# Latent attention in a decoder block: normalized probabilities copied within SBUF and transposed as rounded 32-bit, scores three steps ahead

## The chip, the cores and the metric

The program runs on one core of a Trainium2 chip. The metric is device time of one execution in microseconds (us); lower is better. Three runs of the kernel before took 1321.53, 1325.11 and 1323.86 us, so their median is 1323.86. Engines go by the profile's names: PE multiplies matrices (PEld is its weight load), DVE, ACT and POOL work on vectors, SP issues most transfers. A transfer (DMA) is issued by an engine's instruction and landed by 16 DMA engines.

## The reference

One layer of a decoder block on 1024 tokens of width 1024 in float32: RMS norm, one projection, two attention mixers side by side (a sliding window of 128 keys, and latent attention), gates, an output projection, then a gated feed-forward. The change lies in the latent attention, 8 heads in blocks of 128 queries:

```python
s = (einsum('bqhd,bkhd->bhqk', qn, k_nope) + einsum('bqhr,bkr->bhqk', qr, k_rope)) * scale
s = where(causal, s, -inf)
p = softmax(s, axis=-1)
o = einsum('bhqk,bkhd->bqhd', p, v)
```

## The kernel before

**Products.** The kernel keeps float32 precision by splitting each operand into a rounded high part and a low rest (float32r, "rounded 32-bit", which PE takes at its quick pace) and adding three products: high by high, high by low, low by high. `split` (lines 163 and 166) makes the two parts: a copy on ACT, a subtraction on DVE. Rounded 32-bit operands have four bytes, like float32.

**Stages.** Norm and projections come first, then the sliding-window attention mixed with the gates' projection, then the latent projections, then the latent attention (the stage of the change), then the output products and the feed-forward. The sliding-window part already has a copy of its probabilities within SBUF (`per<-pe`, line 1095) and transposes them as rounded 32-bit (line 1008); so does the stage after it with the latents (`lT`, line 1118).

**The stage of the change.** A loop over t = 0 to 63 (8 heads, 8 query blocks each, in the order 2, 3, 6, 7, 0, 1, 4, 5). Block n of a head has (n+1) x 128 keys. `scores(t)` makes the scores on PE into a buffer `scb` of two PSUM banks, of which there are two buffers; DVE masks them and takes the row maximum (line 1263), ACT takes the exponential and the row sum (1264), POOL inverts the sum (1265) and scales the row (1266) into `p`. `transposes(t)` has PE turn each 128 x 128 block of `p` by a product with the identity matrix (1280) into a PSUM bank `pTb`, and `split` makes of it the halves `pth` and `ptl`. `pv` multiplies these with the values (1302, 1303) into `ob`. In one pass of the loop `scores(t + 2)` is called before `transposes(t)`. Other work fills the loop: products `oA` of the sliding-window output with its output matrix (lines 172 to 174 by `mm3`, ended on DVE at 1359), their weights' loads and splits (`wr`, `wv`), loads of the heads' queries and keys (`qT`, lines 1227 and 1230; `kT`, 1222), gate loads (`sg`, 1333), stores of finished rows (`ar_d`, 1364), and sums of blocks of the output matrix, made by transfers between DRAM tensors `wt_d` (lines 338 and 329).

**What sets the order.** Here no order is written out by hand: a scheduler places every engine's instructions when the program is built, by program order, its own estimate of when inputs are ready, and free slots. Once built, each engine goes through its list in order, and an instruction that has to wait holds up all that stands behind it. SP's list is such a list too, and all its transfers go out through one queue. Tiles called U share 21 slots of 4 KB a partition: `p`, `pth`, `ptl`, and the targets of most loads. PSUM has four banks for `pTb`, `ob`, `oA` and `k` together, and two double banks for `scb`.

Of the kernel before, what the change touches and what calls it, by code (L numbers as in the profile page):

```python
# [8 lines left out]
F32 = mybir.dt.float32  # L9
F32R = mybir.dt.float32r  # L10
# [7 lines left out]
P = 128  # L18
# [71 lines left out]
def hybrid_block_kernel(  # L90
# [29 lines left out]
    nc = tc.nc  # L120
# [9 lines left out]
    def psum_phase(name, bufs):  # L130
        if psum:
            psum.pop("cm").close()
        psum["cm"] = ExitStack()
        psum["x"] = psum["cm"].enter_context(tc.tile_pool(name=name, bufs=bufs, space=PSUM))
# [5 lines left out]
    def uid(name):  # L140
        counter[0] += 1
        return f"{name}_{counter[0]}"

    def U(name, dt=F32, shape=(P, 1024)):
        return pool.tile(list(shape), dt, tag="u", name=uid(name))

    def V(name, dt=F32, shape=(P, 4, 512)):
        return vpool.tile(list(shape), dt, tag="v", name=uid(name))

    def tiny(name, w=1):  # L150
        return small.tile([P, w], F32, tag=f"t{w}", name=uid(name))

    def P1(name, shape=(P, 512), dt=F32):
        return ps1.tile(list(shape), dt, tag="ps", name=uid(name))

    def PX(name, shape=(P, 512), dt=F32):
        return psum["x"].tile(list(shape), dt, tag="ps", name=uid(name))
# [3 lines left out]
    def split(hi, lo, src, eng=None):  # L161

        i = nc.scalar.copy(hi, src)  # L163
        if held[0]:
            tc.keep_in_program_order(i)
        (eng or nc.vector).tensor_tensor(lo, src, hi.bitcast(F32), op=ALU.subtract)  # L166

    def mm3(ps, pairs, first=True, last=True, go_on=False):

        n = len(pairs)  # L170
        for i, ((ah, al), (bh, bl)) in enumerate(pairs):
            nc.tensor.matmul(ps, ah, bh, start=first and i == 0, stop=False, skip_group_check=go_on)  # L172
            nc.tensor.matmul(ps, ah, bl, start=False, stop=False, skip_group_check=go_on)  # L173
            nc.tensor.matmul(ps, al, bh, start=False, stop=last and i == n - 1, skip_group_check=go_on)  # L174
# [7 lines left out]
    def blk(b, n=1):  # L182
        return slice(b * P, (b + n) * P)
# [5 lines left out]
    ident_r = const.tile([P, P], F32R, name="ident_r")  # L189
    ident = ident_r.bitcast(F32)  # L190
# [237 lines left out]
    for g in range(NG):  # L428
        t = V("khd", F32R, (P, 2, S))
# [486 lines left out]
    for b in range(NB):  # L916
# [17 lines left out]
        t = U("lat", F32, (P, C_CKV))  # L934
# [102 lines left out]
    for i, b in enumerate((4, 5, 6, 7, 0, 1, 2, 3)):  # L1037
        ps = P1("kl", (P, KVL))
        mm3(ps, [(hT(k, blk(b)), (wkl[k // 4][0][:, k % 4], wkl[k // 4][1][:, k % 4])) for k in range(NK)])
        t = U("lat", F32, (P, 2, KVL))  # L1040
# [104 lines left out]
    for s in range(2):  # L1145
        pr = P1("krT", (ROPE_B, 4, P), F32R)
        for j in range(4):
            nc.tensor.transpose(pr[:, j], lat[4 * s + j][:, C_RT:C_CKV], ident_r)
        pr = pr.bitcast(F32)
# [63 lines left out]
    def prod_v(b):  # L1213
        ps = P1("v")
        mm3(ps, [((ckv[k][0][:, blk(b)], ckv[k][1][:, blk(b)]), (wv[0][:, k], wv[1][:, k])) for k in range(2)])
        if b % 2 == 0:
            t = V("vM", F32R, (P, 2, NH, P))
            vM.extend([t[:, 0], t[:, 1]])
        split(vM[b][:, :, 0:HD], vM[b][:, :, HD:P], ps.rearrange("p (h d) -> p h d", d=HD))

    def load_k(h):
        nc.sync.dma_start(kT[h % 3][0:64].bitcast(F32), kn_d[h // 2, 64 * (h % 2):64 * (h % 2) + 64])

    def load_q(h):
        if h >= 2:
            qT[h] = V("qT", F32R, (P, 2, S))
            nc.sync.dma_start(qT[h][0:64].bitcast(F32), qn_d[h // 2, 64 * (h % 2):64 * (h % 2) + 64])
        t = qT[h]
        for i in range(2):
            nc.sync.dma_start(t[64 + 16 * i:80 + 16 * i].bitcast(F32), qr_d[i, 16 * h:16 * h + 16])  # L1230

    ob = {}
    live = {}
# [5 lines left out]
    def step(t):  # L1239
        return t // NB, order[t % NB]  # L1240

    def scores(t):
        h, n = step(t)
        w = (n + 1) * P
        sc = PX("scb", (P, 1024))
        qh, ql = (qT[h][0:QK, i] for i in range(2))
        kh, kl = (kT[h % 3][0:QK, i] for i in range(2))
        cw = 320 if w == 640 else 512
        for c0 in range(0, w, cw):
            c1 = min(c0 + cw, w)  # L1250
            kc = slice(c0, c1)
            o = slice(c0 // cw * 512, c0 // cw * 512 + c1 - c0)
            nc.tensor.matmul(sc[:, o], qh[:, blk(n)], kh[:, kc], start=True, stop=False)
            nc.tensor.matmul(sc[:, o], qh[:, blk(n)], kl[:, kc], start=False, stop=False)
            nc.tensor.matmul(sc[:, o], ql[:, blk(n)], kh[:, kc], start=False, stop=True)  # L1255
        nm = tiny("nmb")
        p = U("p")
        den = tiny("denb")
        s_, m_, p_ = sc[:, 0:w], mask[:, S - w:], p[:, 0:w]
        if cw == 320:  # L1260
            s_ = sc.rearrange("p (a c) -> p a c", a=2)[:, :, 0:320]
            m_, p_ = (v.rearrange("p (a c) -> p a c", a=2) for v in (m_, p_))
        nc.vector.tensor_tensor_reduce(s_, s_, m_, 1.0, -NEG, op0=ALU.add, op1=ALU.min, accum_out=nm)  # L1263
        nc.scalar.activation(p_, s_, AF.Exp, scale=-1.0, bias=nm, accum_out=den)  # L1264
        nc.gpsimd.tensor_tensor(den, den, neg_one[:, 0:1], op=ALU.pow)  # L1265
        nc.gpsimd.tensor_scalar(p[:, 0:w], p[:, 0:w], den, 0.0, op0=ALU.mult, op1=ALU.add)  # L1266
        live[t] = p

    def transposes(t):
        h, n = step(t)  # L1270
        p = live.pop(t)
        j, odd = divmod(n, 2)
        if not odd:
            pts[(h, j)] = [(U("pth", F32R, (P, 4, 256)), U("ptl", F32R, (P, 4, 256)))
                           for _ in range((2 * j + 5) // 4)]
        for k0 in range(0, n + 1, 4):
            m = min(4, n + 1 - k0)
            pp = P1("pTb", (P, 4, P))
            for i in range(m):
                nc.tensor.transpose(pp[:, i], p[:, blk(k0 + i)], ident)  # L1280
            hi, lo = pts[(h, j)][k0 // 4]
            split(hi[:, 0:m, blk(odd)], lo[:, 0:m, blk(odd)], pp[:, 0:m])

    def pv(h, j):
        tiles = pts.pop((h, j))
# [45 lines left out]
    def load_sig(i):  # L1331
        gate[i] = U("sg")
        nc.sync.dma_start(gate[i], gate_d[i])

    def twice_sigmoid(g):
        a = nc.scalar.activation(g, g, AF.Tanh, scale=0.5)
        if held[0]:
            tc.keep_in_program_order(a)
# [40 lines left out]
    NT = NH * NB  # L1379
# [34 lines left out]
    prod_k(1, 0)  # L1414
    prod_k(1, 1)
    scores(1)
    prod_v(5)
    prod_v(6)
    prod_v(7)
    load_k(2)  # L1420
    first = {0: (2, 0), 1: (2, 1), 2: (3, 0), 3: (3, 1)}
# [5 lines left out]
    w_at = {t: u[0] // 2 for t, u in fill.items() if u[0] % 2 == 0 and u[1:] == (0, 0)}  # L1427
    g_at = {a: fill[b][0] for a, b in zip([3] + slots, slots) if fill[b][1:] == (0, 0)}
    g_at[NT - 3] = 3
    pvq = []  # L1430
    OUT_AT = {34: 0, 40: 1, 43: 2, 47: 3, 50: 4, 54: 5, 58: 6}
    for t in range(NT):
        h, n = divmod(t, NB)
        if t + 2 < NT:
            scores(t + 2)
        while pvq and pvq[0][0] <= t:
            pv(*pvq.pop(0)[1:])
        if n == 4 and h + 2 < NH:
            load_q(h + 2)
        if n == 6 and h + 3 < NH:  # L1440
            load_k(h + 3)
        hh, nn = step(t)
        if nn % 2 == 1:
            pvq.append((t + 3, hh, nn // 2))
        e = t - (NT - 8)
        if e == 6:
            psum_phase("psc", 4)
        if t in first:
            prod_k(*first[t])
        if t in fill:  # L1450
            dc, sh, c0 = fill[t]
            mix_a(dc, sh, c0, 2, P1("oA") if c0 == 0 else None)
        if t == NT - 1:
            mix_a(13 // 2 ^ 4, 13 % 2, 0, 4, PX("oA"))
        transposes(t)
        if t in OUT_AT:
            out_sums(OUT_AT[t])
        held[0] = True
        if t in g_at:
            load_sig(g_at[t])  # L1460
        if t in fill and fill[t][1:] == (0, 0):
            twice_sigmoid(gate[fill[t][0]])
        if t == NT - 1:
            twice_sigmoid(gate[3])
        if t == 3:
            load_oa(0, 1)
            load_oa(1, 1)
        if t < 4 or 6 <= t < 10:
            split_oa(t % 4 // 2 if t < 4 else (t - 6) // 2, t // 6, t % 2)
        if t + 6 in w_at or t == 0:  # L1470
            st.load_to(st.index[("oa", w_at.get(t + 6, 2))])
        if t + 2 in w_at:
            st.conv_to(st.index[("oa", w_at[t + 2])])
        if e == 4:
            load_sigs(DCS[0])
        if -3 <= e < 3:
            split_ob((e + 3) // 2, (e + 3) % 2)
        if e in (2, 6):
            st.load_to(st.index[("ob", 0 if e == 2 else 2)])
        if e == 6:  # L1480
            st.conv_to(st.index[("ob", 0)])
        held[0] = False
# [234 lines left out]
    lo, hi = half(0), half(1)  # L1717
# [186 lines left out]
    while ffn.n_run < len(ffn.seq):  # L1904
        j, q, m = ffn.run()
# [80 lines left out]
    i = 0  # L1986
# [125 lines left out]
```

## Time and profile before

| what | value |
|---|---|
| runs | 1321.53, 1325.11, 1323.86 us |
| span of the profiled execution | 1323.3 us |
| busy over the span | PE 1310.9 us (99%), DVE 917.0, ACT 634.6, POOL 559.0 |
| granted PE clock, mean | 0.999 |
| the stage of the change | transposes (line 1280) start from 386.0 to 553.1 us |
| transposes in it | 288 of 128 x 128, in 64 steps |
| transfers in the whole program | 245.12 MB, mean 185 GB/s |

The span runs from the first instruction's start to the last one's end; the profiled execution shows no time outside it, and its span lies 0.6 us under the median of the runs. Busy times are unions of instruction spans, and the ends of PE's instructions are modelled: they overlap, so the pace of PE is read from the distances between starts. A row of the timeline gives start, duration, engine, line, operation, out<-in, shape, and in brackets the idle time before it with what ended it. The row of a group of transfers ends with KB each and the median time from issue to landing.

### The profile page before, as it was taken

The numbers are of one execution on the slowest core, as the hardware profiler recorded it, in microseconds if no ns is written. First come the engines' busy times: TensorE is split into PE (matmuls) and PEld (weight loads), VectorE is DVE, ScalarE is ACT, GpSimd is POOL, SyncE is SP. The second block draws the span as 40 slices with busy tenths as digits, with TensorE's granted clock in tenths as the row PEclk, the third lists the DMA queues.
The fourth block names the chain that finished last, engine by engine and source line by source line (L and its number), as shares of the span: only waits on it lengthen the run. The fifth ranks groups of instructions, "written<-read, shape, count | busy, mean of one in ns | idle before, by whom it ended". The sixth has DMA issues, their size and how long they took to land.

```text
span 1323.3 us, 19060 instructions
## 1 busy us (share of the span) xinstructions
PE 1310.9 (99%) x6516; PEld 1103.7 (83%) x6516; DVE 917.0 (69%) x1517; ACT 634.6 (48%) x1282; POOL 559.0 (42%) x619
## 2 busy tenths in 40 slices
PE   9999999999999999999999999999999999999997
PEld 6899888888888889888888888888888888888886
DVE  6868787786767777777779655656666554664863
ACT  7444667665557666755355232323222223644452
POOL 1116545653324556312232465777567631022521
PEclk9999999999999999999999999999999999999999
DMA  9464344456577477898531334655544435996504
GB/s 359 167 195 154 125 162 145 140 184 212 166 241 201 97 223 160 277 322 195 181 122 48 112 130 172 235 195 206 183 181 148 150 112 198 378 376 224 175 17 142
DMA packets 92192, 245.12 MB, mean 185 GB/s; under 512 B 10304, under 2 KB 17984, under 8 KB 90944
## 3 DMA queue, kind: packets, MB, share of 16 engines
q1 hardware_dynamic: 87264, 233.15, 50.9%
q0 software_dynamic: 3392, 8.39, 3.6%
q10 hardware_dynamic: 1440, 2.36, 0.5%
q8 instruction: 52, 0.85, 0.3%
q14 instruction: 44, 0.36, 0.1%
HBM read 161.16 MB, written 78.51 MB: 181 GB/s over the span
## 4 chain that ended last, share of the span: by engine, by line
PE 63%; DVE 2%; issue 1%; POOL 1%; ACT 1%; POOLq 0%; DVEq 0%; ACTq 0%
PE fa L174 6%; PE fa L172 6%; PE fa L173 6%; PE fd L173 5%; PE fd L172 5%; PE fd L174 5%; PE fb L173 5%; PE fb L174 5%; PE fb L172 5%; PE xo L174 2%; PE xo L172 2%; PE xo L173 2%; PE pTb L1280 1%; PE oB L174 1%; PE oB L172 1%
## 5 line engine op out<-in xcount | busy, mean ns | idle before, releaser
L166 DVE TENSOR_TENSOR wl<-wr,wl 128x512 fp32r<-128x512 f32 x150 | 142.5, 973 | 74.7 <-ACT wl L163 74.2
L166 DVE TENSOR_TENSOR lrv<-lr,lrv 128x1024 fp32r<-128x1024 f32 x77 | 105.5, 1401 | 48.2 <-ACT lrv L163 45.6
L163 ACT CAST lrv<-lr 128x1024 fp32r<-128x1024 f32 x77 | 80.2, 1054 | 90.4 <-PE fd L174 56.7
L172 PE MATMUL fd<-lrv 128*128 128x512 f32 x308 | 119.8, 389 | 0.0
L173 PE MATMUL fd<-lrv 128*128 128x512 f32 x308 | 119.8, 389 | 0.0
L174 PE MATMUL fd<-lrv 128*128 128x512 f32 x308 | 119.8, 389 | 0.0
L177 POOL TENSOR_TENSOR wr<-wr,sm 128x512 f32<-128x512 f32 (+1 forms) x38 | 45.5, 1208 | 139.9 <-DVE wl L166 121.7
L163 ACT CAST wl<-wr 128x512 fp32r<-128x512 f32 x150 | 86.7, 621 | 4.8 <-DVE t3l L177 2.8
L166 DVE TENSOR_TENSOR wl<-sm,wl 128x512 fp32r<-128x512 f32 x60 | 50.2, 859 | 42.1 <-ACT wl L163 41.9
L1265 POOL TENSOR_TENSOR denb<-denb,neg_one 128x1 f32<-128x1 f32 x64 | 39.8, 622 | 92.7 <-ACT p L1264 80.7
L172 PEld LDWEIGHTS fd<-lrv 128*128 128x128 f32 x308 | 57.8, 188 | 12.1
L174 PEld LDWEIGHTS fd<-lrv 128*128 128x128 f32 x308 | 57.8, 188 | 12.0
L173 PEld LDWEIGHTS fd<-lrv 128*128 128x128 f32 x308 | 57.8, 188 | 11.9
L1264 ACT ACTIVATE p<-scb,nmb 128x384 f32<-128x384 f32 (+3 forms) x64 | 47.7, 746 | 32.0 <-DVE nmb L1263 23.5
L361 POOL TENSOR_SCALAR ms<-ss 128x1 f32<-128x1 f32 x32 | 8.9, 278 | 125.9 <-ACT xn L1742 47.5
L1263 DVE CUSTOM_DVE_ANT_0 scb<-scb,mask 128x384 f32<-128x384 f32 (+3 forms) x64 | 48.5, 761 | 17.2 <-PE scb L1255 14.6
L1638 ACT ACTIVATE act<-sm 128x512 f32<-128x512 f32 x11 | 7.0, 635 | 102.1 <-DVE sm L180 102.1
L166 DVE TENSOR_TENSOR ptl<-pTb,pth 128x512 fp32r<-128x512 f32 (+2 forms) x96 | 50.0, 550 | 7.9 <-ACT pth L163 7.7
L163 ACT CAST pth<-pTb 128x512 fp32r<-128x512 f32 (+2 forms) x96 | 43.4, 480 | 18.1 <-PE pTb L1280 17.1
L1266 POOL TENSOR_SCALAR p<-p,denb 128x384 f32<-128x384 f32 (+3 forms) x64 | 48.2, 753 | 6.3
L172 PE MATMUL fa<-t1h,wl 128*128 128x512 f32 x120 | 47.1, 392 | 0.4 <-ACT wl L163 0.4
L172 PE MATMUL fb<-t2h,wl 128*128 128x512 f32 x120 | 47.1, 392 | 0.0
(357 smaller groups left out, 4260.7 us busy)
## 6 DMA issues: line engine op xcount, KB each, us to landing
lr<-la_d SPq DMA_DIRECT2D x77, 256.0 KB, 5.4
wr<-in_w_gate_dram SPq DMA_DIRECT2D x22, 512.0 KB, 4.3
wr<-in_w_up_dram SPq DMA_DIRECT2D x22, 512.0 KB, 5.0
la_d<-sd SPq DMA_DIRECT2D x22, 512.0 KB, 5.2
wd<-in_w_down_dram SPq DMA_DIRECT2D x22, 512.0 KB, 6.6
rb_d<-wd SPq DMA_DIRECT2D x22, 512.0 KB, 2.7
lr<-rb_d SPq DMA_DIRECT2D x44, 256.0 KB, 5.4
lr<-in_w_down_dram SPq DMA_DIRECT2D x33, 256.0 KB, 5.4
```

Of the source, the lines that this page charges most:

```text
L163: i = nc.scalar.copy(hi, src)
L166: (eng or nc.vector).tensor_tensor(lo, src, hi.bitcast(F32), op=ALU.subtract)
L172: nc.tensor.matmul(ps, ah, bh, start=first and i == 0, stop=False, skip_group_check=go_on)
L173: nc.tensor.matmul(ps, ah, bl, start=False, stop=False, skip_group_check=go_on)
L174: nc.tensor.matmul(ps, al, bh, start=False, stop=last and i == n - 1, skip_group_check=go_on)
L177: eng.tensor_tensor(out, a, b, op=ALU.subtract)
L361: nc.gpsimd.tensor_scalar(ms, ss, 1.0 / width, EPS, op0=ALU.mult, op1=ALU.add)
L1263: nc.vector.tensor_tensor_reduce(s_, s_, m_, 1.0, -NEG, op0=ALU.add, op1=ALU.min, accum_out=nm)
L1264: nc.scalar.activation(p_, s_, AF.Exp, scale=-1.0, bias=nm, accum_out=den)
L1265: nc.gpsimd.tensor_tensor(den, den, neg_one[:, 0:1], op=ALU.pow)
L1266: nc.gpsimd.tensor_scalar(p[:, 0:w], p[:, 0:w], den, 0.0, op0=ALU.mult, op1=ALU.add)
L1280: nc.tensor.transpose(pp[:, i], p[:, blk(k0 + i)], ident)
```

## The change

The row-scaled `p` is copied by a transfer on SP into a new U tile `pr` of type float32r (the bytes stay the same), `transposes` reads `pr` with the rounded identity, its PSUM tile is float32r, and `split` reads that tile as float32 again. `scores` runs three steps ahead of `transposes` and not two; `scores(2)` is called before the loop.

```diff
         nc.gpsimd.tensor_scalar(p[:, 0:w], p[:, 0:w], den, 0.0, op0=ALU.mult, op1=ALU.add)
-        live[t] = p
+        live[t] = U("pr", F32R)
+        nc.sync.dma_start(live[t].bitcast(F32)[:, 0:w], p[:, 0:w])
...
-            pp = P1("pTb", (P, 4, P))
+            pp = P1("pTb", (P, 4, P), F32R)
             for i in range(m):
-                nc.tensor.transpose(pp[:, i], p[:, blk(k0 + i)], ident)
+                nc.tensor.transpose(pp[:, i], p[:, blk(k0 + i)], ident_r)
             hi, lo = pts[(h, j)][k0 // 4]
-            split(hi[:, 0:m, blk(odd)], lo[:, 0:m, blk(odd)], pp[:, 0:m])
+            split(hi[:, 0:m, blk(odd)], lo[:, 0:m, blk(odd)], pp.bitcast(F32)[:, 0:m])
...
     prod_v(6)
+    scores(2)
     prod_v(7)
...
+    AHEAD = 3
...
-        if t + 2 < NT:
-            scores(t + 2)
+        if t + AHEAD < NT:
+            scores(t + AHEAD)
```

Sixty-four transfers of 64 KB (block 0) to 512 KB (block 7) are new, one a step, 18.9 MB in all (8 heads x 36 blocks x 64 KB). The scheduler places everything anew. Two places show it.

The first is PE at step 25, block 3 of the fourth head: from the last product of its scores (`scb_5246` before, `scb_5260` now) to its transposes (they read `p_5251` before, `pr_5271` now); rows of the same kind are left out. Before:

```order
L1255 MATMUL scb_5246<-kT_4042,qT_4888 128x512
L1253 MATMUL scb_5269<-kT_4042,qT_4888 128x512
...
L1280 MATMUL pTb_5290<-ident_r,p_5204 128x128 x3
L1253 MATMUL scb_5296<-kT_4042,qT_4888 128x512
...
L172 MATMUL oA_5186<-wv_4307,wv_5136 128x512
...
L1280 MATMUL pTb_5317<-ident_r,p_5251 128x128 x4
```

Now:

```order
L1255 MATMUL scb_5260<-kT_4042,qT_4934 128x512
L1281 MATMUL pTb_5298<-ident_r,pr_5180 128x128 x4
L1253 MATMUL scb_5309<-kT_4042,qT_4934 128x512
...
L1281 MATMUL pTb_5332<-ident_r,pr_5213 128x128 x2
L1303 MATMUL ob_5353<-pth_5228,vM_4212 128x256
...
L1281 MATMUL pTb_5360<-ident_r,pr_5245 128x128 x3
L1281 MATMUL pTb_5386<-ident_r,pr_5271 128x128
```

In both, two later sets of scores stand between. Before, six products of `oA` stand there too, and they stand ahead of the scores now; in their place come five more transposes of older steps' rows (14 for 9). The third later set of scores comes only after the first transpose of this step.

The second place is SP's list in the fifth and sixth heads, around the two transfers that start the sums of the output matrix (`wt_d<-in_w_out_dram`, 1 MB each). Before:

```order
L1333 DMA sg_5459<-gate_d 128x1024
L338 DMA wt_d_115<-in_w_out_dram 16x16384
L338 DMA wt_d_117<-in_w_out_dram 16x16384
L1227 DMA qT_5695<-qn_d 64x2048
L1230 DMA qT_5695<-qr_d 16x2048 x2
L239 DMA wr_5670<-in_w_o_swa_dram 128x1024
L1222 DMA kT_4043<-kn_d 64x2048
L1364 DMA ar_d<-sg_5459 128x1024
```

Now, with the copies of steps 37 (`pr_5689`) to 41 (`pr_5838`):

```order
L1268 DMA pr_5689<-p_5683 128x256
L338 DMA wt_d_115<-in_w_out_dram 16x16384
L338 DMA wt_d_117<-in_w_out_dram 16x16384
L1222 DMA kT_4043<-kn_d 64x2048
L1268 DMA pr_5746<-p_5740 128x640
L239 DMA wr_5762<-in_w_o_swa_dram 128x1024
L1365 DMA ar_d<-sg_5536 128x1024
L1268 DMA pr_5778<-p_5772 128x768
L1268 DMA pr_5810<-p_5804 128x384
L1334 DMA sg_5825<-gate_d 128x1024
L1268 DMA pr_5838<-p_5832 128x512
```

The pair stands between the copies of steps 37 and 38, and the loads and stores that the other engines need stand between copies from there on. In the same way the two later transfers `wt_d<-wt_d` stand right ahead of the copies of steps 51 and 58.

## The prediction

> **What bounds the kernel now.** I read the busy times by stage first, then the waits of PE, then the timeline of one step, then the transfers.
>
> ```profile
> 385.00:560.00 175.00, 172.05 (x1098) 150.95 (x1097) 132.79 (x275) 121.13 (x269) 88.64 (x128) 1.00 0.68 190
> 555.00:570.00 15.00, 15.00 (x75) 12.72 (x74) 8.81 (x13) 7.12 (x9) 0.00 (x0) 1.00 1.03 411
> ```
>
> The columns are the stretch, its length, busy us of PE, PEld, DVE, ACT and POOL, the granted clock, the transfers' share and GB/s. In the stage of the change (first row) PE is busy for 172.05 of 175 us at full clock, and the others have a quarter or more free: PE sets the pace. The 16 DMA engines are busy for 0.68 of it. The second row shows them full: 1.03 of their time at 411 GB/s.
>
> ```profile
> PE pTb L1280 <- DVE ob L1314: 0.8, 2, 0.4
> PE oA L173 <- DVE wv L166: 0.7, 2, 0.5
> PE scb L1253 <- ACT p L1264: 0.5, 2, 0.3
> PE ob L1302 <- DVE ptl L166: 0.4, 2, 0.2
> PE oA L174 <- DVE wv L166: 0.3, 1, 0.3
> ```
>
> These are all waits of PE in that stretch: 2.7 us, none of them for the scaled probabilities. So the chain from scores to `p` is hidden behind other work of PE, and a change can win here only by a shorter PE list or by the 2.7 us, and lose where that cover no longer reaches.
>
> **What the transposes cost on PE.** PE's timeline, float32 transposes first, then rounded ones in an earlier stage:
>
> ```profile
> 446.71 0.73 PE L1280 MATMUL pTb<-ident_r,p 128*128 128x128 f32 x5
> 447.19 0.48 PE L1253 MATMUL scb<-kT,qT 96*128 96x512 f32 x1
> 447.51 0.39 PE L1254 MATMUL scb<-kT,qT 96*128 96x512 f32 x1
> 447.74 0.40 PE L1255 MATMUL scb<-kT,qT 96*128 96x512 f32 x1
> 447.97 0.40 PE L1253 MATMUL scb<-kT,qT 96*128 96x512 f32 x1
> ...
> 320.17 0.80 PE L1118 MATMUL lT<-ident_r,lat 128*128 128x128 f32 x8
> 320.81 0.47 PE L172 MATMUL fb<-t2h,wl 128*128 128x512 f32 x1
> 321.12 0.40 PE L173 MATMUL fb<-t2l,wl 128*128 128x512 f32 x1
> ...
> 322.04 0.51 PE L1118 MATMUL lT<-ident_r,lat 128*128 128x128 f32 x4
> 322.39 0.46 PE L173 MATMUL fb<-t2l,wl 128*128 128x512 f32 x1
> 322.69 0.39 PE L174 MATMUL fb<-t2h,wl 128*128 128x512 f32 x1
> ```
>
> Products of 512 columns start every 0.23 us (447.51, 447.74, 447.97), and I take narrower ones in proportion. Five float32 transposes take 0.48 us to the next start, and the product behind them 0.32 and not 0.23: 0.57 in all, 0.11 each. Eight rounded ones take 0.64 and 0.08 extra, 0.72; four take 0.35 and 0.07, 0.42. The difference gives 0.075 for a further rounded transpose and 0.12 for each block of them. Blocks are short: the 288 transposes stand in 82 blocks in the new list. Float32: 288 x 0.11 = 31.7 us; rounded: 288 x 0.075 + 82 x 0.12 = 31.4. So the edit that looks largest is worth about nothing: **term A, -1 us**, with ends -2 and 0.
>
> The Trainium skill ("FP8 and Floating Point Precision", TensorE Precision Notes) says that true float32 takes four passes through the array; by that rule three quarters of the 31.7 us would go and A would be an estimated -24. The rows above do not agree: 0.11 against 0.075 to 0.11.
>
> **What the copy adds to the chain, and what the third step buys.** Rows of step 25 (512 keys) on DVE, ACT, POOL and PE, then of step 27 (1024 keys), then the copies of the sliding-window stage:
>
> ```profile
> 449.37 0.69 DVE L1263 CUSTOM_DVE_ANT_0 scb<-scb,mask 128x512 f32<-128x512 f32 x1
> 450.21 0.69 ACT L1264 ACTIVATE p<-scb,nmb 128x512 f32<-128x512 f32 x1
> 451.72 0.69 POOL L1266 TENSOR_SCALAR p<-p,denb 128x512 f32<-128x512 f32 x1
> 454.03 0.60 PE L1280 MATMUL pTb<-ident_r,p 128*128 128x128 f32 x4
> ...
> 452.42 0.39 PE L1255 MATMUL scb<-kT,qT 96*128 96x512 f32 x1
> 456.28 1.13 POOL L1266 TENSOR_SCALAR p<-p,denb 128x1024 f32<-128x1024 f32 x1
> ...
> DMA to landing us min/median/max: 2.7/3.2/4.5
> per<-pe SPq DMA_DIRECT2D x2, 256.0 KB, 3.6
> lat_d<-lat SPq DMA_DIRECT2D x8, 128.0 KB, 1.7
> ```
>
> Step 25's scores end at 448.14 (447.74 + 0.40) and its `p` at 452.41: 4.3 us. Step 27's are 452.81 and 457.41: 4.6. For the narrowest block I take 3.5. PE turned step 25's rows 1.6 us after they were ready.
>
> The copy lies behind that. An SBUF copy of 512 KB landed 2.7 to 4.5 us after its issue, median 3.2; for smaller ones the nearest rows are 3.6 (256 KB) and 1.7 (128 KB, to DRAM). No copy of 64 KB was traced; I take 1.8 rising to 3.2 with the block, and keep 0.3 less and 0.6 more as ends. So a step needs 5.3 us (block 0) to 7.8 us (block 7) from the last score product to the first transpose.
>
> Against that stands PE work between the two in the new list, summed by the pace above for all 64 steps: 8.2 us on average, 6.1 before. The third step thus buys 2.1 us and not a whole step (some 2.6), and the copy costs 2.5. On average 8.2 is enough for 6.6, but it is uneven. At step 25 there are nine score products of 512 columns (2.0 us), three of 384 (0.5), four small `ob` (0.4) and 14 transposes in five blocks (1.6): 4.5 us, where 4.3 + 2.5 = 6.8 is needed. Going through the list and counting a stall once for all steps that it helps, eleven of 64 steps fall short: 9, 10, 17, 25, 29, 33, 34, 41, 51, 58 and 62, by 2.4 (25), 1.5 (41), 1.4 (29), 1.2 (33) and less than 1 each for the rest. **Term B, +10 us**, with ends 7.5 (copies 0.3 quicker) and 16 (0.6 slower).
>
> **What stands ahead of the copies in SP's queue.** Here are SP's issues in one stretch (start, time of the issue, transfer), and the transfers' time to landing there:
>
> ```profile
> 465.16 0.34 SPq L1364 DMA_DIRECT2D ar_d<-sg  x1
> 465.59 0.38 SPq L1333 DMA_DIRECT2D sg<-gate_d  x1
> 466.03 1.32 SPq L338 DMA_DIRECT2D wt_d<-in_w_out_dram  x2
> 467.39 0.89 SPq L1227 DMA_DIRECT2D qT<-qn_d  x1
> 468.32 1.08 SPq L1230 DMA_DIRECT2D qT<-qr_d  x2
> 472.52 0.35 SPq L239 DMA_DIRECT2D wr<-in_w_o_swa_dram  x1
> ...
> qT<-qr_d SPq DMA_DIRECT2D x2, 128.0 KB, 12.2
> wr<-in_w_o_swa_dram SPq DMA_DIRECT2D x1, 512.0 KB, 9.5
> wt_d<-wt_d SPq DMA_DIRECT2D x2, 6.8
> ...
> SPq L1364 <- DVE sg L1359: 32.3, 4, 14.9
> ```
>
> A transfer of 128 KB issued behind the `wt_d` pair landed after 12.2 us, one of 512 KB issued four us later still took 9.5: transfers of this queue land one behind the other. Of the 12.2 us some 2.5 are its own, 1.3 each are the 512 KB of `qT`, of `sg` and of the `ar_d` ahead of it (at 411 GB/s), so the pair holds the queue for about 5.5 us. In the new list the copy of step 38 follows that pair and a `kT` load. It is issued about 2 us after the pair, so it lands some 5 us late; step 38 has 7.4 us of PE work for 7.0 needed, so PE waits 4.5 us; `wr` and `ar_d` ahead of step 39's copy add about 1. The two `wt_d<-wt_d` ahead of the copies of steps 51 and 58 take 6.8 us to land where a copy alone takes 3; with a step of 2.6 us (64 steps from 386.0 to 553.1) between issues they make those copies 1 to 2 us late, and both steps are short already: 2 us. Each copy also waits on SP for POOL's scaling, and the `qT`, `kT`, `sg` and `wr` loads behind it wait with it; they are needed many steps later. The other way round `ar_d` waits there for DVE's gate product (last row: four waits, 32.3 us), and now the copies of steps 13, 21, 28 and 39 wait behind it; PE's products for it stand 4 us and more ahead of those steps' transposes, and most steps behind `qT` and `sg` have 2 us to spare: 0.5 us. **Term C, +8 us**, with ends 0 (the pair goes out early enough) and 19 (each of these holds the next two copies too).
>
> The Trainium skill ("DMA: Bandwidth & Descriptors", Queues, rings and completion order) says that completion is not first-in, first-out for an issuing engine, a later transfer may finish before an earlier one; if the copies overtook what stands ahead, C would be an estimated 0. The rows here show no overtaking.
>
> The copies' bytes also fill the DMA engines: 18.9 MB at 411 GB/s are 46 us of their time, 0.26 of the stage, 0.94 with the 0.68 there is. I price nothing more for that; it is the third rival.
>
> **What is taken away or hidden.** Of PE's 2.7 us of waits about 2 end inside the new stalls, since DVE and ACT catch up while PE stands: **term D, -2 us**, ends -2.7 and 0. The issue time of the 64 copies, half a microsecond each on SP, is hidden because SP only waits and issues. The loads for the next stage now stand behind the copies of steps 61 to 63 and go out some three steps, 8 us, later; the last `oA` and the first `oB` products hide them (24 of 512 columns each, 5.5 us a set); without that cover they would cost up to 8. The two score buffers stay two, so `scores(t + 3)` waits for step t + 1's exponential, as `scores(t + 2)` did for step t's; the distance on PE hardly changes, 0 to +2, taken as 0.
>
> **Sum.** -1 + 10 + 8 - 2 = +15. The span is 1323.3 and lies 0.6 under the median of the runs: **1338 us**. By the ends the mechanism gives 1327 (-2 + 7.5 + 0 - 2.7) to 1359.
>
> **Rivals.** An execution that differs by under 0.3%, 4 us, can't be told from no change here.
>
> *The covered copy (faster).* At every short step the chain is quicker than I took it, since scores issued earlier meet idle DVE and ACT, and all copies land under the longer lead; then only the gains are left: 1 to 2 us of A, all 2.7 of D, and up to 4 us if the 0.12 per block shrinks where transposes follow products of the same type. The time would be 1323.9 - 6 = 1318. It decides if step 25's chain falls from 6.8 to 4.5. For it: 1.6 us of slack before the transposes now. Against: step 27's 4.6 us is mostly the four instructions themselves.
>
> *No change.* The short steps cost 5 us, the pair of `wt_d` goes out while the copies have slack, and A and D give 4 back: 1325. For it: the scheduler counts with some time for a copy, and most steps have 1.5 us left. Against: step 25 as listed.
>
> *The queue binds (much slower).* At 0.94 of the DMA engines the copies wait like the loads did from 466 to 482, for 5 us and more on most steps; a lead of 8.2 then misses 9.5 by over a microsecond every second step: some +40, 1363. For it: 12.2 us above. Against: the engines' spare third is spread over all of the stage.
>
> *The change doesn't do what it says*: if the transposes stayed float32, A alone would be 0; I give it no chance of its own.
>
> **How the numbers follow.** Forecast 0.53, covered copy 0.20, no change 0.14, queue binds 0.13. Slower by over 4 us: 0.53 + 0.13 = 0.66; within 4 us 0.14; faster 0.20. The forecast's own range is 1328 to 1354. The range for 8 in 10 takes in no change and the inner half of the other two: 1317 to 1358.
>
> **What would show it.** Right: PE's waits in the stage rise from 2.7 to some 15 us, most of them ahead of line 1281 and ended by the transfer `pr<-p`; the longest stand at steps 38 and 39 (behind `wt_d`) and at 25, 29, 33 and 41; the transposes' starts lie 0.075 us apart with a gap behind each block. Wrong: no wait of line 1281 on a transfer (then the leads did suffice), a copy behind the `wt_d` pair that lands within 4 us (no queueing), or a rise of the stage's length with the waits on POOL or DVE instead. Outside the stage nothing should move.

## The result, and the profile after

The changed kernel takes 1378.71 us (median; 1374.72 to 1381.38), the kernel before 1323.65 us beside it: 1.042 times as long, with an interval of 1.0399 to 1.0442. The prediction had 1338 and a range up to 1358: the direction was right, and the loss came out at 55 us instead of 15. The profiled execution has a span of 1376.3 us.

The first question is where the 55 us lie. The two kernels, each cut at the end of the last transposes; the columns are those of the prediction's first fence (stretch, length, busy us of PE, PEld, DVE, ACT, POOL, granted clock, share of the 16 DMA engines, GB/s). Before:

```profile
386.00:553.00 167.00, 164.05 (x1054) 144.06 (x1053) 128.74 (x270) 118.08 (x263) 88.64 (x128) 1.00 0.67 180
553.00:1323.00 770.00, 763.54 (x3408) 632.28 (x3406) 499.26 (x593) 292.30 (x451) 318.89 (x246) 1.00 0.53 186
```

After:

```profile
385.00:606.00 221.00, 185.85 (x1047) 158.41 (x1045) 126.99 (x267) 117.61 (x261) 87.02 (x128) 0.86 0.77 224
606.00:1376.00 770.00, 763.25 (x3409) 632.63 (x3407) 503.83 (x593) 292.02 (x451) 316.97 (x246) 1.00 0.53 185
```

All of it lies in the stage of the change, which grew from 167 to 221 us; what follows takes 770 us in both. The 54 us have two parts: PE is idle for 35.2 us instead of 3.0, and it is busy for 21.8 us longer, at a granted clock of 0.86 instead of 1.00, though the rounded transposes leave it some 4 us less to do (shown below).

The idle part, from PE's waits after the change (total us, times, longest):

```profile
PE pTb L1281 <- DMA pr<-p: 27.0, 14, 3.8
PE pTb L1281 <- DVE ptl L166: 2.7, 6, 0.8
```

Seven of the stops as PE's timeline shows them (start, duration, and in brackets the idle time ahead with what ended it):

```profile
393.09 1.02 PE L1281 MATMUL pTb<-ident_r,pr 128*128 128x128 f32 x7 [3.72 <-DMA pr<-p]
...
414.91 0.59 PE L1281 MATMUL pTb<-ident_r,pr 128*128 128x128 f32 x3 [3.76 <-DMA pr<-p]
...
463.50 0.51 PE L1281 MATMUL pTb<-ident_r,pr 128*128 128x128 f32 x4 [2.85 <-DMA pr<-p]
...
517.05 0.34 PE L1281 MATMUL pTb<-ident_r,pr 128*128 128x128 f32 x2 [1.29 <-DMA pr<-p]
...
520.57 0.72 PE L1281 MATMUL pTb<-ident_r,pr 128*128 128x128 f32 x4 [1.63 <-DMA pr<-p]
...
540.24 0.34 PE L1281 MATMUL pTb<-ident_r,pr 128*128 128x128 f32 x1 [2.53 <-DMA pr<-p]
...
600.58 0.72 PE L1281 MATMUL pTb<-ident_r,pr 128*128 128x128 f32 x4 [3.52 <-DMA pr<-p]
```

PE stands before the transposes and the copy releases it, 14 times. Counted by the transposes, these are steps 2, 7, 22, 38, 39, 44 and 62. What stood ahead of step 7's copy: SP's issues (start, duration):

```profile
403.02 0.52 SPq L1211 DMA_DIRECT2D kn_d<-kns  x1
403.64 1.43 SPq L1323 DMA_DIRECT2D oar<-oa_d  x2
405.15 0.49 SPq L1227 DMA_DIRECT2D qT<-qn_d  x1
406.77 0.50 SPq L1268 DMA_DIRECT2D pr<-p  x1
```

And the times from issue to landing of those issued from 404.2 to 407.2 (the last number of a row):

```profile
oar<-oa_d SPq DMA_DIRECT2D x1, 512.0 KB, 6.0
qT<-qn_d SPq DMA_DIRECT2D x1, 512.0 KB, 7.7
pr<-p SPq DMA_DIRECT2D x1, 384.0 KB, 8.0
```

A store and three loads of 512 KB each went out within 3.8 us, and the copy behind them landed after 8.0 us. Unblocked copies take about 3 (512 KB: median 3.2). The DMA engines in two such stretches:

```profile
455.00:463.00 8.00, 5.65 (x34) 4.74 (x32) 4.15 (x10) 4.55 (x12) 4.80 (x7) 1.00 1.03 226
463.00:472.00 9.00, 7.08 (x30) 5.58 (x30) 4.29 (x8) 2.71 (x6) 0.75 (x2) 0.61 0.98 183
```

They are full (0.98 and 1.03), yet move only 183 and 226 GB/s, where the prediction had counted with 411. Loads of `qT` and `kT`, which write 64 of the 128 partitions or fewer (lines 1222 to 1230), pass there. By the trace's packet records their packets of 8 KB take 0.61 us each in the stage (median), where packets of 4 KB in SP's queue take 0.16. The Trainium skill ("SBUF — State Buffer", Door 1: The DMA port swizzle) says that a transfer into partitions 0 to 63 reaches only half of the memory's DMA ports, some 218 GB/s at most; the rows come near that, with other transfers among these loads.

Not all of the backlog stands in SP's queue, and not all of it is loads. Step 44's copy (64 KB) was issued at 532.22 with one older copy ahead of it in SP's queue, which landed at 533.03. It landed 7.9 us after its issue. Just before, POOL had issued one of its four sums of the output matrix (line 329, 1 MB each) in its own queue:

```profile
529.98 1.14 POOL L329 DMA_DIRECT2D wt_d<-in_w_out_dram  x1
...
532.22 0.47 SPq L1268 DMA_DIRECT2D pr<-p  x1
...
pr<-p SPq DMA_DIRECT2D x1, 64.0 KB, 7.9
...
q0 software_dynamic: 113, 0.46, 98.0%
```

The last line is all that the DMA engines did from 533.4 to 535.9: POOL's queue (q0) has 98.0% of their time for 0.46 MB (185 GB/s), and SP's queue moves nothing. The copies of steps 47, 54 and 62 were also under way together with such a sum. The stops at these four steps (2.53, 1.84, 0.80 and 3.52 us) are 8.7 of the 27.0 us.

The busy part: PE's timeline around the stop at 414.91:

```profile
410.25 0.39 PE L1255 MATMUL scb<-kT,qT 96*128 96x512 f32 x1
410.47 0.34 PE L1253 MATMUL scb<-kT,qT 96*128 96x384 f32 x1
...
416.41 0.63 PE L1255 MATMUL scb<-kT,qT 96*128 96x512 f32 x1
416.84 0.63 PE L1253 MATMUL scb<-kT,qT 96*128 96x512 f32 x1
417.27 0.63 PE L1254 MATMUL scb<-kT,qT 96*128 96x512 f32 x1
...
421.03 0.39 PE L174 MATMUL oA<-wv,wv 128*128 128x512 f32 x1
421.25 0.39 PE L172 MATMUL oA<-wv,wv 128*128 128x512 f32 x1
```

The stretches around it, and one after two shorter stops:

```profile
413.00:414.00 1.00, 0.00 (x0) 0.00 (x0) 0.48 (x1) 0.00 (x0) 0.00 (x0) 0.87 0.71 102
414.00:420.00 6.00, 5.09 (x20) 4.43 (x21) 3.13 (x7) 3.42 (x8) 1.56 (x2) 0.50 0.74 158
420.00:421.00 1.00, 1.00 (x6) 0.89 (x6) 0.58 (x2) 1.00 (x3) 0.00 (x0) 0.72 0.17 68
...
523.00:531.00 8.00, 8.00 (x38) 7.06 (x37) 4.86 (x9) 5.67 (x11) 4.74 (x6) 0.58 0.16 61
```

Products of 512 columns start 0.22 us apart ahead of the stop and behind 421, and 0.43 apart between (416.41, 416.84, 417.27): the clock falls to 0.50 some 2.6 us into the stop (0.87 in 413 to 414) and comes back in 420 to 421 (0.72), 6.8 us in all, 5.7 of them full of work. So behind a stop of 3.76 us PE takes nearly 3 us longer for the same work. The Trainium skill ("TensorE: Matmul & The Clock Gate", What's actually happening) says that an idle window of about 3.4 us puts PE on half clock until a window of work releases it; this trace agrees on the half clock and on its release by work, with 6.8 us for two such windows, but not on the idle window: the clock fell after 2.6 us of idleness. Two shorter stops close together did the same: 1.29 us ahead of 517.05 and 1.63 ahead of 520.57, and the clock in 523 to 531 is 0.58 with PE busy throughout.

### The profile page after: what moved, and what is told of

The parts are those of the page before. It is cut to its first block, busy times and chain, and to the rows that moved or that the text cites. A ratio compares the mean times of both kernels' runs of the same rounds, so it can differ in the third digit from the quotient of the medians.

```text
span 1376.3 us, 19222 instructions
## 1 busy us (share of the span) xinstructions
PE 1331.4 (97%) x6516; PEld 1118.5 (81%) x6516; DVE 921.2 (67%) x1517; ACT 634.7 (46%) x1282; POOL 556.0 (40%) x619
## 4 chain that ended last, share of the span: by engine, by line
PE 70%; issue 11%; POOL 7%; DMA 5%; DVE 5%; ACT 2%; SPq 0%; POOLq 0%; DVEq 0%; ACTq 0%
PE fa L172 8%; PE fa L174 8%; PE fa L173 8%; PE fb L172 6%; PE fb L173 6%; PE fb L174 6%; PE fd L174 5%; PE fd L172 5%; PE fd L173 5%; POOL p L1266 3%; POOL denb L1265 2%; DMA pr<-p 2%; PE xo L174 2%; PE xo L172 2%; PE xo L173 2%
## 5 line engine op out<-in xcount | busy, mean ns | idle before, releaser
L166 DVE TENSOR_TENSOR wl<-wr,wl 128x512 fp32r<-128x512 f32 x150 | 145.3, 992 | 73.3 <-ACT wl L163 72.8
L1281 PE MATMUL pTb<-ident_r,pr 128*128 128x128 f32 x288 | 40.5, 260 | 32.9 <-DMA pr<-p 27.0
L1281 PEld LDWEIGHTS pTb<-ident_r,pr 128*128 128x128 f32 x288 | 34.0, 150 | 46.4 <-issue 23.6
L172 PEld LDWEIGHTS fd<-lrv 128*128 128x128 f32 x308 | 57.8, 188 | 11.8
```

The lines of the kernel that those rows point to most:

```text
L1281: nc.tensor.transpose(pp[:, i], p[:, blk(k0 + i)], ident_r)
```

## The experiments

Each run is told with its median and its ratio to runs of the kernel before beside it. The theory, W: copies land late behind loads, PE stands for them, and its clock falls behind the stops.

### Which part of the change costs

The third step alone:

```diff
-        if t + 2 < NT:
-            scores(t + 2)
+        if t + 3 < NT:
+            scores(t + 3)
```

> The kernel before with scores(t + 3) and scores(2) ahead of the loop; no copy, float32 transposes. Theory W (the copies land late, PE stands before the transposes, and behind such a stop PE's clock is granted low for some microseconds): without the copy nothing is late, 1322 us, 1318 to 1326, no wait of the transposes over 1 us, clock 1.00 in the stage. Rival S (the third step alone makes it slower, by the new order of the lists or by the tiles it holds): 1340 to 1378.

Measured: 1323.98 us, 1.0004 (0.9994 to 1.0013). The third step costs nothing by itself and brings nothing.

The copy with float32 transposes:

```diff
-        live[t] = U("pr", F32R)
-        nc.sync.dma_start(live[t].bitcast(F32)[:, 0:w], p[:, 0:w])
+        live[t] = U("pr")
+        nc.sync.dma_start(live[t][:, 0:w], p[:, 0:w])
...
-                nc.tensor.transpose(pp[:, i], p[:, blk(k0 + i)], ident_r)
+                nc.tensor.transpose(pp[:, i], p[:, blk(k0 + i)], ident)
```

> The changed kernel with the copy and the third step, but pr and the transposes' PSUM tile in float32 and the plain identity. Theory W: the type does not matter for the waits, 1379 us, 1372 to 1386, waits ahead of the transposes of 25 us or more. Rival T (the rounded transposes are what slows PE or its clock): 1323 to 1335.

Measured: 1379.29 us, 1.042 (1.0396 to 1.0444). The type makes no difference to the loss.

Rounded transposes without the copy:

```diff
-        nc.gpsimd.tensor_scalar(p[:, 0:w], p[:, 0:w], den, 0.0, op0=ALU.mult, op1=ALU.add)
         live[t] = U("pr", F32R)
-        nc.sync.dma_start(live[t].bitcast(F32)[:, 0:w], p[:, 0:w])
+        nc.gpsimd.tensor_scalar(live[t][:, 0:w], p[:, 0:w], den, 0.0, op0=ALU.mult, op1=ALU.add)
```

> The changed kernel without the copy: POOL's scaling writes the tile pr of type float32r itself, so that p loses the bits below the rounding there (that part of the precision is left out); transposes rounded, scores three steps ahead. Theory W with term A of the prediction (rounded transposes are worth 1 us in these short blocks): 1322 us, 1318 to 1326. Rival (rounded transposes cost a quarter of float32 ones): some 1300.

Measured: 1324.39 us, 1.0008 (0.9996 to 1.002). PE's stage in the run with the third step alone (first row) and in this one:

```profile
386.00:553.00 167.00, 164.24 (x1051) 143.88 (x1050) 127.42 (x268) 116.92 (x262) 87.19 (x127) 1.00 0.68 180
```

```profile
385.00:551.00 166.00, 160.42 (x1050) 139.26 (x1048) 126.31 (x266) 116.93 (x262) 86.52 (x127) 1.00 0.65 176
```

PE has 3.8 us less to do and stands 2.8 longer (5.6 idle for 2.8). The rounded form makes PE's list shorter, and the kernel's time stays the same, as the prediction said; float32 transposes at four times the price are ruled out, as that would show as some 24 us. So the copy is the whole of the loss.

### The queue, or the engines behind it

```diff
-        nc.sync.dma_start(live[t].bitcast(F32)[:, 0:w], p[:, 0:w])
+        nc.gpsimd.dma_start(live[t].bitcast(F32)[:, 0:w], p[:, 0:w])
```

> The changed kernel with the 64 copies issued by POOL, right behind its scaling, in POOL's own queue and not in SP's. Theory Q (the copies are late because they stand behind loads in SP's one queue, and the loads behind copies that wait for POOL): most of the 27 us of waits on pr go, 1325 to 1345. Rival E (the 16 DMA engines themselves are full in those stretches, whatever the queue): the waits stay, 1365 to 1385.

Measured: 1400.11 us, 1.0581 (1.0533 to 1.063), slower still. One place in this run, from the timelines of SP and of POOL:

```profile
494.51 1.74 SPq L338 DMA_DIRECT2D wt_d<-in_w_out_dram  x2
...
495.85 0.61 POOL L1268 DMA_DIRECT2D pr<-p  x1 [0.41 <-POOL p L1266]
```

And the times to landing of what was issued from 495.7 to 496.0, by queue:

```profile
pr<-p POOLq DMA_DIRECT2D x1, 384.0 KB, 11.8
wt_d<-in_w_out_dram SPq DMA_DIRECT2D x1, 9.8
```

Ahead of it in POOL's queue stood only the copy before, which landed 0.7 us after this one's issue, and yet it took 11.8 us; the second transfer of the `wt_d` pair, issued just ahead of it from SP, took 9.8, so that the copy landed 2 us behind it. Here a queue of its own did not let the copy pass what the engines had already taken on.

The same with ACT's queue (`nc.scalar.dma_start`):

> The changed kernel with the 64 copies issued by ACT in ACT's own queue. ACT stands for POOL's scaling before each, 1.2 to 1.7 us, so its casts for the transposes come later; SP's list is as before. Theory E (the engines behind the queues are full of loads): copies issued behind a burst still land after 6 to 12 us, also from another queue, and the time is 1355 to 1395. Rival Q (the queue shared with the loads made them late): copies land within 4 us everywhere, 1325 to 1345.

Measured: 1414.89 us, 1.0705 (1.0689 to 1.0721). The copies' median times to landing, and ACT's waits:

```profile
pr<-p ACTq DMA_DIRECT2D x8, 512.0 KB, 2.9
...
pr<-p ACTq DMA_DIRECT2D x8, 384.0 KB, 6.6
pr<-p ACTq DMA_DIRECT2D x8, 320.0 KB, 5.6
```

```profile
ACT p L1264 <- POOL p L1266: 24.2, 12, 2.4
ACT otb L1309 <- POOL p L1266: 17.2, 9, 2.0
```

Here too the copies of steps that fall behind bursts land late (medians of 6.6 and 5.6 us for 384 and 320 KB, where 512 KB take 2.9), and ACT stands for POOL ahead of each issue, with its casts behind it. Both runs speak for the engines and against the shared queue as the cause, as does step 44 in the changed kernel, with the queues the other way round.

Next, less in the engines. Only the first 128 columns copied and waited for:

```diff
-        nc.sync.dma_start(live[t].bitcast(F32)[:, 0:w], p[:, 0:w])
+        nc.sync.dma_start(first_b[:, 0:P], p[:, 0:P])
...
+                nc.tensor.transpose(pp[:, i], (p if k0 + i else first_b)[:, blk(k0 + i)], ident)
```

> Three steps ahead, float32 transposes; only the first 128 columns of each row (64 KB) are copied, and only the transpose of block 0 reads the copy, the others read p. So every step waits for a copy as in the changed kernel, but with 4.2 MB of copies instead of 18.9. Theory E (a copy lands when the loads issued ahead of it have gone through the 16 DMA engines, whatever its own size): stops of 15 to 25 us stay behind the bursts of loads, 1360 us, 1348 to 1372. Rival B (the copies' own bytes fill the engines): 1324 to 1340.

Measured: 1365.07 us, 1.0312 (1.0294 to 1.0329), with 17.4 us of waits on `pr<-p`. A copy of 64 KB still keeps three quarters of the loss: it waits for what is ahead of it.

Without the loads of queries and keys:

```diff
-            qT[h] = V("qT", F32R, (P, 2, S))
-            nc.sync.dma_start(qT[h][0:64].bitcast(F32), qn_d[h // 2, 64 * (h % 2):64 * (h % 2) + 64])
+            qT[h] = qT[h - 2]
+            return
```

> The changed kernel without the loads of queries for heads 2 to 7 and of keys for heads 3 to 7 (those heads use the tiles of earlier heads, so that part of the computation is left out): 7.2 MB of loads less in the stage. Theory E (the stops stand behind bursts of loads): the stops at 415, 463 to 473, 540 and 565 us go, about half of the 35 us of idle PE and of the low clock: 1350 us, 1338 to 1360. Rival P (the chain with its 2 to 3 us copy is too long for the lead, loads or not): 1368 to 1382.

Measured: 1358.77 us, 1.0263 (1.0247 to 1.0278), with 17.5 us of waits on `pr<-p`: 20 us better than the change, at the upper edge of what theory E gave. Of these waits 9.9 us are left at steps 44, 47, 54 and 62, where POOL's sums are again under way; the longest, with its sum:

```profile
521.04 0.95 POOL L329 DMA_DIRECT2D wt_d<-in_w_out_dram  x1
...
533.85 0.60 PE L1283 MATMUL pTb<-ident_r,pr 128*128 128x128 f32 x3 [4.78 <-DMA pr<-p]
```

So these loads are one part of the backlog and POOL's sums seem to be another; no run is without the sums.

Those loads in pieces of 4 KB a packet:

```diff
+            for i in range(2):
+                nc.sync.dma_start(qT[h][0:64, i].bitcast(F32), qn_d[h // 2, 64 * (h % 2):64 * (h % 2) + 64, i])
```

> The changed kernel with each of those loads of 512 KB issued as two of 256 KB, so that a packet has 4 KB and not 8. In the changed kernel's trace 8 KB packets take 0.55 to 0.66 us each and 4 KB packets 0.16 to 0.21. Theory E with that price: the loads' time in the engines falls by a third and the stops behind them by 5 to 10 us: 1371 us, 1362 to 1376. Rival (the packets' size does not matter): 1377 to 1384.

Measured: 1377.65 us, 1.0403 (1.0388 to 1.0419). My price was wrong: the packets' size does not matter. It fits half of the ports as the limit, but that was not tried by itself.

### A shorter and a longer lead

`AHEAD = 2`, 4 and 5 in the changed kernel, with as many `scores` calls before the loop:

> The changed kernel with scores two steps ahead instead of three. By its list the PE work between a step's last score product and its first transpose is 6.5 us on average, 8.2 in the changed kernel. Taking the changed kernel's 64 distances from scores to landing (mean 9.5 us, longest 17) against these leads, stops add up to 89 us of PE time, 62 with the leads of the changed kernel. Theory W/E (late landing against lead): 1379 + 26 = 1405, 1390 to 1425. Rival (the third step itself brings nothing or harms): 1370 to 1385.

Measured: 1381.0 us, 1.0441 (1.0422 to 1.046), against my forecast. Its waits on `pr<-p` are 35.1 us for 27.0, but the time is only 2 us longer. Why the shorter lead costs so little is left open.

> The changed kernel with scores four steps ahead. Its list has 10.0 us of PE work between scores and transposes. By the same sum the stops fall from 62 to 31 us: 1379 - 32 = 1347, 1335 to 1360. Rival U (more rows in flight take tiles from the loads, which then come late and in larger bursts): no better than 1365.

Measured: 1368.03 us, 1.0337 (1.032 to 1.0354). PE's waits:

```profile
PE pTb L1281 <- DVE ob L1315: 12.4, 12, 2.3
PE pTb L1281 <- DMA pr<-p: 3.8, 2, 3.7
```

> The changed kernel with scores five steps ahead: 12.5 us of PE work between. By the same sum 7 us of stops are left, and the ones that are left are under 3 us, so that the clock stays at 1.00: 1324 to 1336, forecast 1328. Rival U (tiles): above 1345.

Measured: 1353.64 us, 1.0232 (1.0216 to 1.0247). A longer lead takes the waits on the copy away as theory W says (27.0, then 3.8, then 2.3 us), but the time does not follow: with four steps PE stands for DVE instead. Something else costs some 20 to 30 us even where PE hardly waits for a copy. With five steps ACT waits for copies in its place:

```profile
ACT p L1264 <- DMA pr<-p: 13.6, 5, 4.5
```

The exponential does not read `pr`. What it can wait for is the tile that it writes to, if a copy holds that tile until it lands.

### Copies that nobody waits for

```diff
+        live[t] = p
+        spare = U("pr")
+        nc.sync.dma_start(spare[:, 0:w], p[:, 0:w])
```

> Scores three steps ahead, and the same 64 transfers on SP, but into spare tiles that nothing reads; PE turns the float32 p itself, as before. Theory W (all of the 55 us is PE standing for the copy's landing, and the low clock behind such stops): with nobody waiting the time is 1324 us, 1319 to 1331, and the clock 1.00 in the stage, though the DMA engines are as full as in the changed kernel. Rival D (the copies' traffic itself is what costs, by making loads that others need late, or by holding tiles): 1340 to 1378.

Measured: 1344.52 us, 1.0161 (1.0143 to 1.0178). Theory W in its pure form falls: 21 us come without any wait of PE on a copy. PE's and ACT's waits there:

```profile
PE oA L172 <- ACT wv L163: 3.4, 2, 2.8
PE pTb L1282 <- DVE ptl L166: 1.9, 2, 1.1
```

```profile
ACT sg L1338 <- DMA sg<-gate_d: 7.9, 5, 4.0
...
ACT pth L163 <- DMA pr<-p: 2.8, 2, 1.8
...
ACT p L1264 <- DMA pr<-p: 1.3, 2, 0.9
```

Many small waits, and gate loads that ACT now stands for. ACT also waits 4.1 us for the landing of copies that nothing reads, which again can only be for tiles. Three more pairs divide the 21 us. The copy cut to 16 columns (`spare[:, 0:16]`), on SP and on POOL:

> As the run with unread copies (1344.5 us, 21 more than before, with no wait on a copy), but each spare copy takes 16 columns (8 KB) instead of the whole row; the 64 issues on SP, their waits for POOL and the spare tiles stay. Theory T (the 21 us come from the copies' bytes, which make the loads that ACT and DVE work on land late): 1324 us, 1319 to 1331. Rival L (they come from SP's list, where loads now stand behind copies that wait for POOL, and from the tiles held): 1338 to 1348.

Measured: 1336.92 us, 1.0099 (1.0084 to 1.0114). Bytes are a third of the 21 us, not all.

> The run with unread copies of 16 columns, issued by POOL in its own queue instead of by SP. Theory L (the 14 us come from SP's list): 1324 to 1329. Rival M (they come from the spare tiles, from tiles that are released only when a transfer has read them, or from the scheduler's new order): 1333 to 1342.

Measured: 1333.01 us, 1.0085 (1.0068 to 1.0102), 10.7 more than before beside it; SP's list is at most a small part.

Then 8 columns into a small tile outside the 21 shared ones (`spare = tiny("spare", 8)`), again on SP and on POOL:

> The run with tiny unread copies issued by SP (1336.9 us, 14 more than before), but the copy takes 8 columns into a small tile of its own pool, so that no second one of the 21 shared tiles is held. Theory H (the held tile is what costs, loads and casts wait for a free one): 1324 to 1329. Rival L (SP's list and the order of the engines): 1333 to 1339.

Measured: 1329.97 us, 1.0051 (1.0033 to 1.0069), 7.1 more than before.

> The run with tiny unread copies issued by POOL (1333.0 us, 11 more than before), with the same small tile. Theory H: 1323 to 1327. Rival L: 1330 to 1335, from POOL's issues (0.6 us each and 0.4 us of waiting) and from the new order.

Measured: 1327.3 us, 1.003 (1.0018 to 1.0041), 4.4 more. Both rivals were half right: the copy's own shared tile costs 6.5 us on SP and 6.3 on POOL; the issues with the new order cost 7.1 and 4.4. A second shared tile alone is not it: the run with POOL's rounding takes one a step too, without a transfer, and loses nothing. That a landing holds back the next user of a tile is what ACT's waits above show; that this makes up the 6 us is argued, not shown.

So the 55.1 us divide, by differences of runs: 7.1 for the 64 issues on SP and the order that follows, 6.5 for the tile held, 7.1 for the bytes (20.7 - 13.6), and the rest, 34.4, for PE waiting on the landing and its low clock. By the intervals each of these differences is uncertain by 2 to 3 us, each run has an order of its own, and nothing shows that the parts simply add.

### What the low clock costs by itself

At the eight steps ahead of the longest stops, the transpose of block 0 is repeated, 20 and 40 times:

```diff
+            if t in (1, 6, 21, 38, 43, 46, 50, 61) and k0 == 0:
+                for _ in range(20):
+                    nc.tensor.transpose(pp[:, 0], p[:, blk(0)], ident_r)
```

> The changed kernel with the transpose of block 0 repeated 20 times (same result) at the eight steps that stand just ahead of the longest stops: 8 x 20 x 0.075 = 12 us more work for PE, put where it stands 1.6 to 3.8 us. Theory C (the granted clock falls behind stops, and that costs some 20 us): shorter stops leave more of the stage at full clock, and with more work the time falls: 1362 to 1377. Rival N (the clock costs nothing of its own, the stops set the time): the filling is absorbed, 1377 to 1383. Rival (the filling adds to the path): 1385 to 1392.

Measured: 1380.33 us, 1.0452 (1.0417 to 1.0488).

> The same with 40 repeats, 24 us more work, of which the stops can take 19. Theory C: stops under 1 us are left at those places, the clock stays up there, 1360 to 1376. Rival N: 1381 to 1388. Rival (on the path): 1395 to 1404.

Measured: 1380.46 us, 1.0436 (1.0414 to 1.0458). The stage with 20 repeats:

```profile
385.00:606.00 221.00, 192.92 (x1208) 166.87 (x1207) 129.08 (x268) 118.42 (x263) 87.23 (x128) 0.90 0.76 222
```

Twelve microseconds of work went in, PE's busy time rose by only 7.1, and the clock rose from 0.86 to 0.90: some 5 us of the work were paid by the clock, the rest by idle time. Theory C wanted a time below that of the change, and neither median is; 40 repeats (24 us) cost 2 us in the median. It seems that with less low clock PE only meets the late copies sooner. The filling was of transposes alone; products in their place were not tried. What the clock costs by itself is therefore not settled: the 21.8 us of slower work and the 35 us of idle PE stand partly for each other.

No version here beats the kernel before; the rounded transposes without a copy equal it.

## Why the prediction was right in its sign and wrong in its size

The sum had 18 us for waits on the copy (terms B and C) and nothing for copies that nobody waits for. By the differences of runs, the waits and their slow stretches took 34 us, and 21 came without any wait of PE on a copy. (From 1323.9 the sum of +15 is 1339 and not 1338; that does not matter here.)

- **"Lose where that cover no longer reaches"**: right; that is what happened, and outside the stage nothing moved, as said.
- **Term A (-1)**: right for the time, 1379.29 for 1378.71 with the copy, 1323.98 for 1324.39 without. Its own figures, 31.7 and 31.4, give -0.3; PE's list became 3.8 us shorter, beyond the ends, and PE stood for most of that. The estimate of -24 that went by the Trainium skill's four passes ("FP8 and Floating Point Precision") is out.
- **Term B (+10, eleven short steps)**: the steps were mostly the wrong ones. Of the eleven, 10, 25, 51 and 62 are among the 14 waits for copies; 9, 17, 29, 33, 34, 41 and 58 are not. Of the five longest stops, steps 2, 7, 22, 44 and 62, only the last was on the list; the others had leads of 8.1 to 10.8 us. The failed input is the need of 5.3 to 7.8 us, built from unblocked copies: from the last score product to landing, the 64 steps of the trace took 9.5 us on average and up to 17 (5.0 to `p`, where 3.5 to 4.6 were taken, and 4.4 from issue to landing, where 1.8 to 3.2 were). Against that even leads of 10.0 and 12.5 us (four and five steps) leave something.
- **Term C (+8)**: this is the step that failed. It priced copies only behind SP's `wt_d` transfers and gave 0.5 us to "most steps behind `qT` and `sg`". The pair cost steps 38 and 39 stops of 1.29 and 1.63 us, not 5.5: step 38's copy went out more than 7 us behind it, not 2. The later two cost 2.19 at step 51 and nothing at 58, for 2. Behind loads of `kT` and `qT`, steps 2, 7 and 22 had stops of 3.72, 3.76 and 2.85 us, 10.3 in all against that 0.5. POOL's four sums, which C leaves out, were under way at four more stops, 8.7 us. Two errors lie under it: half a megabyte of `qT` was priced at 1.3 us by 411 GB/s, where the engines move 183 and 226 with such loads; and the mechanism was one queue's order, where the copies were late from POOL's and ACT's queues too, and SP's copies late behind POOL's transfers.
- **Term D (-2) and what was called hidden**: wrong. PE's other waits in the stage did not shrink by 2 us, they grew from 2.7 to 7.5. "Needed many steps later", said of the loads behind the copies, "hidden", said of the issues, and "I price nothing more for that", said of the bytes, stand against 20.7 us in the run with unread copies; the tiles that the copies hold were not priced at all.
- **Not in the prediction**: the clock. The trace before has no stop of PE over a microsecond in the stage and 1.00 throughout, so nothing there showed it; but a forecast of stops of 3 us and more left open what follows a stop.
- **The rivals**: "the queue binds" (1363, chance 0.13) was the nearest. Its lag of 9.5 us against 8.2 is what was measured on average. That is in part luck: it had the copies late by 5 us and more on most steps, and about half of them landed within 3.6 us; the others came late in bursts. It was turned down because the DMA engines' "spare third is spread over all of the stage"; the prediction's own second row, 1.03 at 411 GB/s in 555 to 570, and the 12.2 us landings of `qT` showed that it comes in bursts. The covered copy and no change are out.
- **What would show it**: waits mostly ahead of line 1281 and ended by `pr<-p`: right in kind, 27.0 us for 15; the longest at 2, 7 and 62, not at 38, 39, 25, 29, 33 and 41.

## What to carry to other kernels

An average share of the DMA engines says nothing of a short transfer on the critical path: look for the windows in which they are full, and add to its own time the whole backlog there, at the rate that those transfers really reach, whatever queue issues it. A transfer put into a hidden chain costs even when it is never late, by the tile it holds and the loads that now stand behind it: 21 of 55 us here. And behind a stop of PE of some 3 us a slow stretch is to be looked for; what that costs by itself was not settled here.

## What the runs showed that was not expected

- PE's granted clock fell to 0.50 some 2.6 us into a stop of 3.76 us and came back after 6.8 us; stops of 1.29 and 1.63 us within 5 us did it too.
- A copy of 384 KB in a queue of its own took 11.8 us, with 2 MB issued from another queue up to 1.3 us before.
- A copy of 64 KB in SP's queue took 7.9 us while POOL's queue had 98% of the DMA engines' time at 185 GB/s.
- Engines at 0.98 to 1.03 of their time moved between 183 and 412 GB/s, and splitting the 64-partition loads into packets of half the size changed nothing.
- PE took 24 us of extra work in the stage for 2 us of time in the median.
